# Finishing the last sample unit's pending results in turns

## The chip, the cores and the metric

The kernel runs on one core of one Trainium2 chip. The metric is the device time of one execution in microseconds. Five engines run their own queues, each in order: TensorE (PE, with its weight loads PEld), VectorE (DVE), ScalarE (ACT), GpSimd (POOL) and SyncE (SP). ACT, SP and POOL also issue DMA transfers from their queues.

## The reference

One encoder layer is applied to two sequences with the same weights: a sample of 1024 tokens and a prompt of 512. All is float32.

```python
h = rms_norm(x, norm_g)                 # width 2048
z = h @ w_in                            # 2048 -> 5632: c_val, c_glu, c_gate, q, k, v, a_gate
conv = conformer_conv(c_val, c_glu, ...) * silu(c_gate)   # 31 taps, layer norm, 1024x1024 product
attn = banded_sink_attention(rope(q), rope(k), v, sink) * silu(a_gate)  # 8 heads, window 128
y = rms_norm(x + concat[conv, attn] @ w_out, final_norm_g)
```

A gate's path, which matters here, is short: a product with `w_in`, a scaling by the token's RMS factor, a SiLU, and a store to device memory.

## The kernel before, in words

**Products.** Every float32 product is made of three matmuls on halves: an operand is split into a high part (`hi`, an ACT copy or scaling) and a low part (`lo`, a DVE subtraction), and hi x hi, hi x lo and lo x hi are accumulated. `parts` (L506 to L515) writes such a split. Weights are loaded as `raw` tiles (3 buffers) and split into `hl` tiles (3 buffers); tokens live split in `t` tiles (28 buffers).

**Units, for the sample.** `Unit` (L94) makes two blocks of 128 columns of `w_in` times 1024 tokens over half of the 16 blocks of inputs, in Strassen's way: seven products (steps 0 to 6, order P1, P2, P6, P5, P7, P3, P4) of 4 blocks x 3 matmuls of 128x512 each, so 12 matmuls a step (`product`, L193, matmuls at L207). After a step its sum is taken off PSUM by `tap` (L230); that work is late, that is, it is traced in the next step behind its first three matmuls. Four results come out of a unit, named by token half and column block: (0,0) after P2, (1,1) after P7, (0,1) after P3 and (1,0) after P4.

**Pending results.** A unit over the second half of the inputs must add the partial result of the first half, which waits in device memory. `finish` (L260) issues an accumulating DMA from the POOL queue (`add_into`, L501: tile `g` or `u` <- `part_...`, 256 KB) and appends an entry to the list `later`: a counter, `landing` (4 for most units), and a generator with the rest of the work. For a gate the generator is `silu_of` (L976): first the scaling on DVE (`scaled`, L975), and at the next call the SiLU on ACT (L983) and the store to `gate_d` (L984); for the last gates the store is issued on ACT's own queue. The tiles `g` and `u` have four buffers each and are also used by the rotation of queries and keys, by the attention's query loads (L1150) and others.

**Turns.** `turn_over` (L542) counts down every entry of `later`, and calls the generator of each whose counter has come to zero; one call a turn. In a unit there is a turn in each step, behind the first three matmuls and the late work. `turn_over(True)` calls all of them, whatever their counter. What a turn traces has priority (`high_priority(URGENT)`), so the planner that orders each engine's instructions may put it ahead of up to some 400 instructions traced before it.

**Marks.** `turn_over` also calls `mark` (L523), which remembers the last DVE and the last ACT instruction traced so far. What is traced within `behind` (L534) is queued on those engines behind the marks. All steps of the three background lanes (`conv`, `attn`, `prep`; class `Lane`, L64) run within `behind`: the convolution's taps, the attention, and preparations. Lanes are advanced by `tick`, as time is counted while the matmuls are traced. The order on an engine comes from the planner, by priority and by what it takes to be ready, within these bounds.

**Jobs, for the prompt.** `Job` (L386) makes one block of 128 columns times 512 tokens over 16 blocks of inputs (`k`), 3 matmuls each, so 48 (L670); the jobs with `w_pw` have 8 blocks. `run` (L641) goes through all items: the sample's units, the prompt's 44 jobs (keys and values first, then queries, then convolution and gates), 16 jobs with `w_pw` for the sample, the units with `w_out`, and 8 jobs with `w_pw` for the prompt; a last stage follows. At each half of a job, behind its first three matmuls, the next weights are prepared (`w_prep`) and there is one turn. The late work of the job before comes behind the first three matmuls of a job. Before each job, `later` is emptied by forced turns (L657, L658).

**Around the boundary.** `end` is the sample's last unit with `w_in`, two gate blocks. During its steps 0 to 3 it also splits the prompt's 16 token blocks (`follow`, L2018: an ACT scaling at L514 and a DVE operation at L515 for each, four blocks a step), into the `t` tiles that its own tokens leave. Its `landing` is 8. The prompt's first two jobs make the keys and values of head group 0 (weights split at L510 and L511, or, where the low part was kept in device memory, at L418 and L420), and the sample's attention starts beside them (L1131, L1161, L1169 on).

Of the kernel before, what the change touches and what calls it, by code (L numbers as in the profile page):

```python
# [45 lines left out]
NT, NRAW, NHL = 28, 3, 3  # L46
OWN = 12
FILLS = {(0, 1, 2): 2, (1, 0, 0): 3}
HALF = 4
# [381 lines left out]
class Encoder:  # L431
# [209 lines left out]
    def run(self, items):  # L641

        nc = self.nc
        late = []
        for n, item in enumerate(items):
            for x in item:
                for fn in x.before:
                    fn()
            if isinstance(item[0], Unit):
                for u in item:  # L650
                    u.alone = len(item) == 1
                    u.open()
                for step in range(len(item[0].STEPS)):
                    for u in item:
                        late = u.product(step, late)
                continue
            while self.later:  # L657
                self.turn_over(True)  # L658
            job = item[0]
            job.acc = [self.acc()]  # L660
            nk = len(job.ks)
            for q in range(0, nk, 2 * HALF):
                at = job.at + q // (2 * HALF)
                self.w_prep(at + 1)
                hl = self.hl.pop(at)
                for kk in range(2 * HALF):
                    i = q + kk
                    hi, lo = job.rhs(job.ks[i])
                    for p, (l, r) in enumerate(((0, hi), (0, lo), (1, hi))):
                        nc.tensor.matmul(  # L670
                            job.acc[0],
                            hl[:, l, kk // HALF, kk % HALF, :],
                            r,
                            start=i == 0 and p == 0,
                            stop=i == nk - 1 and p == 2,
                        )
                    if kk == 0:
                        self.w_prep(at + NHL - 1)
                        self.turn_over()
                    if i in job.ticks:  # L680
                        job.ticks[i]()
                    self.tick(3 * MM)
                    if i == 0:
                        for fn in late:
                            fn()
                        late = []
            late = [lambda job=job: self.urgently(job.evac, job.acc)]
        for fn in late:
            fn()
# [1185 lines left out]
def encoder(ctx, tc, a):  # L1875
# [152 lines left out]
            load_two(j)  # L2028

    end = stages[3][-1]  # L2030
    end.look, end.landing = NHL - 1, 8
    end.before.append(last_before)
    for step in range(4):
        end.after[step] = [lambda step=step: follow(step)]
# [143 lines left out]
```

## Time and profile before

| | us |
|---|---|
| runs, median (lowest to highest) | 2078.87 (2078.43 to 2080.28) |
| the profiled execution | 2079.13 |
| its span | 2077.4 |
| PE busy | 2060.1 |
| DVE busy | 1728.4 |
| ACT busy | 1081.8 |
| POOL busy | 157.9 |

The span is the part of the execution that the trace covers; the rest of its time lies around it. A row of a timeline gives the start, the time from the first instruction's start to the last one's end, the engine, the line, the operation, the tiles written and read, their count, and in brackets how long the engine was idle before it and what ended that. SPq, ACTq and POOLq are DMA issues on those queues. Matmuls are pipelined, so that a row of several is longer than their number times the distance between two by the length of one's tail. A row of waits gives engine, line and tile that waited, what it waited for, and the total, the count and the longest, in us.

### The profile page before, as it was taken

What the parts mean: (1) busy time and instruction counts of PE and PEld (TensorE: products, weight loads), DVE (VectorE), ACT (ScalarE), POOL (GpSimd) and SP (SyncE); (2) the same over time, 40 slices, a digit from 0 to 9 for tenths busy, and PEclk for the clock granted to TensorE, in tenths of its full rate; (3) what the DMA queues carried; (4) which work ended last, traced back from release to release, by engine and by line L of the source; (5) the groups of instructions that cost most, each with busy time, mean ns of one, the idle gap of its engine ahead of it and who ended that gap; (6) DMA issues with size and microseconds to landing.
All of it is one profiled execution on the core that took longest, in us unless ns stands there. A gap on an engine that the chain in (4) does not pass through costs nothing.

```text
span 2077.4 us, 27223 instructions
## 1 busy us (share of the span) xinstructions
PE 2060.1 (99%) x9256; PEld 1697.9 (82%) x9256; DVE 1728.4 (83%) x2843; ACT 1081.8 (52%) x1771; POOL 157.9 (8%) x240
## 2 busy tenths in 40 slices
PE   9999999999999999999999999999999999999998
PEld 8888888888888888788888888888888887888886
DVE  8768899998899899889766777776799978998877
ACT  7486445333465555655555777336553343454454
POOL 0111111111112111100000000000000111100000
PEclk9999999999999999999999999999999999999999
DMA  8888886864577777954555555997789898778897
GB/s 285 309 300 256 200 215 226 286 218 158 190 243 197 181 167 179 279 167 158 164 183 185 178 172 188 316 329 233 239 295 295 279 324 283 213 259 277 293 324 279
DMA packets 242300, 494.56 MB, mean 238 GB/s; under 512 B 23664, under 2 KB 84464, under 8 KB 242160
## 3 DMA queue, kind: packets, MB, share of 16 engines
q1 hardware_dynamic: 216352, 428.83, 62.1%
q0 software_dynamic: 24512, 61.88, 12.5%
q10 hardware_dynamic: 1296, 2.11, 0.3%
q8 instruction: 72, 1.18, 0.2%
q14 instruction: 68, 0.56, 0.1%
HBM read 331.77 MB, written 160.96 MB: 237 GB/s over the span
## 4 chain that ended last, share of the span: by engine, by line
PE 73%; issue 8%; DMA 8%; DVE 7%; ACT 2%; POOL 1%; SPq 0%; ACTq 0%; POOLq 0%; DVEq 0%
PE a L207 21%; PE a L670 13%; PE c L207 10%; PE b L670 6%; PE c L670 6%; PE b L207 5%; PE s L1169 2%; PE pv L1198 2%; PE a L1852 2%; PE s L207 2%; DVE hl L511 2%; PE pt L1203 1%; PE s L1852 1%; DVE t L511 1%; DMA p<-y_d 1%
## 5 line engine op out<-in xcount | busy, mean ns | idle before, releaser
L207 PE MATMUL a<-t,hl 128*128 128x512 f32 x2640 | 632.5, 390 | 1.8 <-ACT u L236 1.3
L207 PEld LDWEIGHTS a<-t,hl 128*128 128x128 f32 x2640 | 493.5, 188 | 108.4 <-ACT u L236 2.4
L511 DVE TENSOR_TENSOR hl<-raw,hl 128x1024 fp32r<-128x1024 f32 (+3 forms) x334 | 337.8, 1012 | 151.5 <-ACT hl L510 147.3
L510 ACT ACTIVATE hl<-raw 128x1024 fp32r<-128x1024 f32 (+3 forms) x334 | 296.8, 889 | 314.4 <-PE c L207 88.1
L670 PE MATMUL a<-t,hl 128*128 128x512 f32 x1344 | 326.3, 393 | 0.0
L207 PE MATMUL c<-t,hl 128*128 128x512 f32 x1320 | 319.1, 389 | 0.0
L670 PEld LDWEIGHTS a<-t,hl 128*128 128x128 f32 x1344 | 248.8, 188 | 50.4
L207 PEld LDWEIGHTS c<-t,hl 128*128 128x128 f32 x1320 | 247.4, 188 | 51.5 <-DVE u L304 0.2
L1041 DVE SCALAR_TENSOR_TENSOR f<-f,c_w_dw,f 128x512 f32<-128x512 f32 x248 | 172.9, 744 | 0.2
L670 PE MATMUL b<-t,hl 128*128 128x512 f32 x672 | 162.9, 392 | 1.5 <-DVE t L515 0.8
L670 PE MATMUL c<-t,hl 128*128 128x512 f32 x672 | 163.9, 393 | 0.0
L1004 DVE SCALAR_TENSOR_TENSOR f<-f,c_w_dw,f 128x512 f32<-128x512 f32 x232 | 163.4, 742 | 0.2
L207 PE MATMUL b<-t,hl 128*128 128x512 f32 x660 | 159.8, 389 | 0.0
L670 PEld LDWEIGHTS b<-t,hl 128*128 128x128 f32 x672 | 124.8, 188 | 27.5 <-DVE t L515 1.1
L670 PEld LDWEIGHTS c<-t,hl 128*128 128x128 f32 x672 | 124.6, 188 | 24.8
L207 PEld LDWEIGHTS b<-t,hl 128*128 128x128 f32 x660 | 123.7, 188 | 25.6
L1033 DVE SCALAR_TENSOR_TENSOR f<-f,w_both,f 128x512 f32<-128x512 f32 x120 | 89.8, 748 | 2.0
L236 ACT ACTIVATE u<-a 128x512 f32<-128x512 f32 x82 | 48.8, 595 | 77.3 <-PE a L207 70.6
L236 ACT ACTIVATE g<-a 128x512 f32<-128x512 f32 x78 | 46.5, 596 | 78.5 <-PE a L207 68.5
L1183 ACT ACTIVATE p<-p,tiny 128x384 f32<-128x384 f32 (+1 forms) x96 | 54.6, 570 | 45.9 <-DVE tiny L1180 36.2
L510 ACT ACTIVATE a<-pt 128x512 fp32r<-128x512 f32 x64 | 38.0, 593 | 64.6 <-PE pt L1203 64.4
L285 POOL DMA_DIRECT2D g<-xT_s x16 | 8.8, 551 | 743.1 <-DMA att_d<-u 669.0
(356 smaller groups left out, 2765.2 us busy)
## 6 DMA issues: line engine op xcount, KB each, us to landing
raw<-w_in SPq DMA_DIRECT2D x170, 512.0 KB, 5.2
raw<-w_out SPq DMA_DIRECT2D x31, 512.0 KB, 5.1
raw<-w_pw SPq DMA_DIRECT2D x24, 512.0 KB, 4.2
wsum_P<-raw SPq DMA_DIRECT2D x47, 256.0 KB, 3.6
raw<-wsum_P SPq DMA_DIRECT2D x18, 512.0 KB, 5.1
f<-x_s SPq DMA_DIRECT2D x16, 512.0 KB, 8.5
g<-wsum_P SPq DMA_DIRECT2D x28, 256.0 KB, 4.6
a<-sum_S SPq DMA_DIRECT2D x24, 256.0 KB, 6.1
```

The costliest lines, as they stand in the source:

```text
L207: nc.tensor.matmul(acc, hl[:, l, o, j, :], toks[j][:, r], start=name in FRESH and j == 0 and q == 0, stop=name in LAST and j == HALF - 1 a ...
L236: nc.scalar.activation(t, bank, AF.Copy)
L510: nc.scalar.activation(hi, x, AF.Copy)
L511: nc.vector.tensor_tensor(lo, x, hi.bitcast(F32), ALU.subtract)
L670: nc.tensor.matmul(job.acc[0], hl[:, l, kk // HALF, kk % HALF, :], r, start=i == 0 and p == 0, stop=i == nk - 1 and p == 2,)
L1004: nc.vector.scalar_tensor_tensor(t, h[:, j : j + T], w(j), t, ALU.mult, ALU.add)
L1033: nc.vector.scalar_tensor_tensor(m0, odd[:, j : j + H], both(j), m0, ALU.mult, ALU.add)
L1041: nc.vector.scalar_tensor_tensor(out, d[:, j : j + H], w(2 * j + k), out if j else m0, ALU.mult, ALU.add)
L1169: nc.tensor.matmul(ps[:, 0:n], qs[:, x, h], k[y][:, keys], start=p == 0, stop=p == 2)
L1183: nc.scalar.activation(p[:, 0:n], p[:, 0:n], AF.Exp, bias=nm[:, h : h + 1], accum_out=l[:, h : h + 1])
L1198: nc.tensor.matmul(pv, v[x][:, vs], pt[:, y], start=i == 0 and p == 0, stop=i == last and p == 2)
L1852: nc.tensor.matmul(acc[t], self.toks[name, m][:, x, i, t * P : (t + 1) * P], parts[i][l].rearrange("p a b -> p (a b)"), start=fresh and fi ...
```

## The change

Three lines change. The forced turns before each job go. In a job there is a turn at every fourth block of inputs, where before there was one at every eighth. And the `landing` of the sample's last unit becomes 5 in place of 8. What is pending when a job begins stays in `later` and is finished in that job's or the next one's turns.

```diff
@@ def run
                         late = u.product(step, late)
                 continue
-            while self.later:
-                self.turn_over(True)
             job = item[0]
             job.acc = [self.acc()]
...
                     if kk == 0:
                         self.w_prep(at + NHL - 1)
+                    if kk % HALF == 0:
                         self.turn_over()
                     if i in job.ticks:
                         job.ticks[i]()
@@ def encoder
     end = stages[3][-1]
-    end.look, end.landing = NHL - 1, 8
+    end.look, end.landing = NHL - 1, 5
     end.before.append(last_before)
```

`HALF` is 4. The loop `for kk in range(2 * HALF)` runs over the eight blocks of a half of a job.

## The prediction

> **What bounds the kernel now.** I read the page's busy shares first, then the busy time by stretches, because the change touches one place in the middle.
>
> ```profile
> span 2077.4 us, 27223 instructions
> PE 2060.1 (99%) x9256; PEld 1697.9 (82%) x9256; DVE 1728.4 (83%) x2843; ACT 1081.8 (52%) x1771; POOL 157.9 (8%) x240
> ```
> ```profile
> 856.00:870.00 14.00, 12.55 (x53) 9.52 (x52) 8.34 (x11) 8.61 (x12) 0.88 (x1) 1.00 1.05 318
> 870.00:900.00 30.00, 30.00 (x146) 24.92 (x145) 22.08 (x45) 16.82 (x30) 0.00 (x0) 1.00 0.60 196
> 900.00:1000.00 100.00, 100.00 (x472) 82.92 (x471) 90.38 (x164) 53.35 (x101) 0.00 (x0) 1.00 0.50 164
> 1200.00:1400.00 200.00, 198.66 (x912) 162.99 (x911) 145.13 (x247) 104.60 (x163) 0.00 (x0) 1.00 0.74 250
> 1800.00:1910.00 110.00, 110.00 (x490) 90.61 (x489) 99.51 (x154) 56.51 (x86) 5.50 (x10) 1.00 0.77 254
> ```
>
> The columns are the stretch, its length, then PE, PEld, DVE, ACT, POOL busy, the granted clock and the DMA's share and rate. TensorE is the bound nearly everywhere. Its one marked hole in the middle is 856 to 870 us, where the prompt's first job runs: 14.00 - 12.55 = 1.45 us. The timeline of PE shows it in steps.
>
> ```profile
> 833.63 5.60 PE L207 MATMUL a<-t,hl 128*128 128x512 f32 x24
> 839.07 2.88 PE L207 MATMUL b<-t,hl 128*128 128x512 f32 x12
> ...
> 856.03 0.61 PE L670 MATMUL b<-t,hl 128*128 128x512 f32 x2
> 857.14 10.67 PE L670 MATMUL b<-t,hl 128*128 128x512 f32 x44 [0.49 <-DVE hl L511]
> 868.63 0.73 PE L670 MATMUL b<-t,hl 128*128 128x512 f32 x2 [0.82 <-DVE t L515]
> 869.20 6.30 PE L670 MATMUL a<-t,hl 128*128 128x512 f32 x27
> ```
>
> Undisturbed, 24 matmuls take 839.07 - 833.63 = 5.44 us, 0.2267 us each. The first job's 48 should take 10.88 us and take 869.20 - 856.03 = 13.17: 2.29 us lost. Of that, 1.11 - 0.45 = 0.66 us goes at the start, for the first weight's low part (L511), and the other 1.63 us later, mostly for the last token split (L515). The chain of waits tells why that split is late.
>
> ```profile
> 855.03 6.64 DMA u<-part_gate
> 861.68 0.03 issue
> 861.70 0.70 DVE u L975
> 862.40 0.02 issue
> 862.43 0.64 ACT u L983
> ...
> 864.12 0.90 ACT hl L418
> ...
> 865.71 0.96 ACT hl L510
> ...
> 867.83 0.76 DVE t L515
> ```
>
> So the 256 KB accumulating load of a pending result, issued at 855.03, lands at 861.67. The scaling on DVE (L975) and the Silu on ACT (L983) stand in the queues in front of the splits. DVE and ACT show the rest.
>
> ```profile
> 857.00 0.68 DVE L975 TENSOR_TENSOR g<-g,f 128x512 f32<-128x512 f32 x1
> 860.18 0.69 DVE L975 TENSOR_TENSOR u<-u,f 128x512 f32<-128x512 f32 x1 [2.50 <-DMA u<-part_gate]
> 861.70 0.69 DVE L975 TENSOR_TENSOR u<-u,f 128x512 f32<-128x512 f32 x1 [0.83 <-DMA u<-part_gate]
> 862.31 0.75 DVE L515 SCALAR_TENSOR_TENSOR t<-a,c_norm_g,t 128x512 fp32r<-128x512 f32 x1
> ...
> 869.63 0.68 DVE L975 TENSOR_TENSOR g<-g,f 128x512 f32<-128x512 f32 x1
> ```
> ```profile
> 860.91 0.63 ACT L983 ACTIVATE u<-u 128x512 f32<-128x512 f32 x1 [2.56 <-DVE u L975]
> 862.43 0.63 ACT L983 ACTIVATE u<-u 128x512 f32<-128x512 f32 x1 [0.89 <-DVE u L975]
> 863.19 0.89 ACTq L984 DMA_DIRECT2D gate_d<-u  x2
> 865.61 1.04 ACT L510 ACTIVATE hl<-raw 128x1024 fp32r<-128x1024 f32 x1
> 866.56 0.71 ACT L514 ACTIVATE t<-a,c_norm_g 128x512 fp32r<-128x512 f32 x1
> ```
>
> DVE idles 2.50 + 0.83 = 3.33 us on the two landings, ACT 3.45 us behind it, and ACT then issues two stores (0.89 us). The last split's ACT half starts only at 866.56.
>
> **The change part by part.** *The forced finish goes.* In place of two rounds at the job's start, the results come in turns, one every 12 matmuls, and the first, (0,0), reaches its fifth turn in the unit's last step. Its scaling stands behind the first weight's low part, where it is at 857.00 already: cost 0, and the 0.66 us at the start stay. (1,1) is scaled at the ninth k of job 0, 22 matmuls behind 857.14, 862.1 us; its load had landed by 860.18. (0,1) comes 12 matmuls on, at 864.8, landed by 861.67. (1,0), with a load issued a little later, comes in the second job, after 870, where 869.63 showed no wait. Three scalings (0.69 us), three Silus (0.63) and their stores on ACT's own queue move behind the splits; none is added. What was queued behind them, the last splits, needs 0.75 us of DVE each and can be done before 861, while PE wants the last at matmul 46, near 866.9. Gain: the 1.63 us.
>
> *What is late next.* The second job starts at 857.14 + 46 x 0.2267 = 867.57 instead of 869.20, so its weights (L510 at 865.61, then 1.23 us of L511) must keep up. If L418 still starts at 864.12, L511 ends near 867.9, and the third matmul wants it at 868.02. That weight goes into the buffer that job 0's first half frees at 862.1, so no earlier. I take off 0.2 us for this, bounds 0 (L418 earlier) and 1.63 (job 2 not ready before 869.20): net gain 1.4, between 0 and 1.6. I stay near the upper end because the Silu and store issue, 0.63 + 0.89 us, no longer stand before L418.
>
> *Buffers.* The waiting results hold their u and g tiles some 5 to 7 us longer. Of four u tiles two are held, one is the query's and one the rotation's; the next query load (SP) wants one when the first query has been read. If it had to wait, the weight loads behind it on SP would slip by up to 3 us, but the third job's weight has more margin than that.
>
> ```profile
> 865.83 0.69 DVE L511 TENSOR_TENSOR a<-u,a 128x512 fp32r<-128x512 f32 x1
> 875.95 1.23 DVE L511 TENSOR_TENSOR hl<-raw,hl 128x1024 fp32r<-128x1024 f32 x1 [2.31 <-ACT hl L510]
> 881.70 5.61 PE L670 MATMUL c<-t,hl 128*128 128x512 f32 x24
> ```
>
> The low part ends at 877.18 and PE wants it at 881.70 or, with the gain, 880.3: 3 us of cover. Cost 0; without the cover the whole slip, up to 3 us.
>
> *The marks.* Every turn also renews the point behind which the background lanes (convolution, attention, preparation) are ordered. The 44 prompt jobs have two halves, the 24 later ones one: 112 turns become 224. No instruction is added; the order on DVE and ACT tightens in all jobs. No trace shows its price. From below: nothing, or a gain up to the idle PE has left between 900 and 1910 us, of which the row 1200 to 1400 has the most, 1.34 us. From above, see the slower rival. I take 0, since 1800 to 1910 has DVE 90% busy and no idle PE.
>
> *Other pending results.* The second sample stage's last output squares also lose their forced finish; they need one turn only, and PE is full there (1800 to 1910): 0.
>
> *The sum.* The profiled execution took 2079.13 us, 1.73 around its span. 2079.13 - 1.4 = 2077.7; the runs' median, 2078.87, is 0.26 lower: **2077.5 us**.
>
> **A rule against the trace.** The loads above took 6.6 to 7 us from issue to landing. The Trainium skill, DMA: Bandwidth & Descriptors, Anatomy of one DMA, fits 2.0 us plus bytes over 436e3 per us for this path; an estimate from that page for 262,144 bytes is 2.6 us. By that rule both loads would have landed by 857.7, the forced finish would wait for nothing, and the change would bring nothing, 2078.9. The DVE rows disagree: 860.18 and 861.70.
>
> **The rivals.** *The wait stays (2078.9).* Turns are urgent: the planner may put a scaling ahead of its turn, if it thinks the load has landed, and a split behind it again. For: the mark alone fixes how early, and (1,1) has only 862.1 - 860.18 = 1.9 us in hand. Against: it now stands behind the second job's weight, which is late itself. Gain 0 to 0.4.
>
> *The lanes are pinned (slower).* Attention's parts between transposes and products have no margin:
>
> ```profile
> 1017.89 0.60 PE L1203 MATMUL pt<-c_ident,p 128*128 128x128 f32 x4
> 1019.71 0.93 PE L1198 MATMUL pv<-a,t 128*128 128x512 f32 x3
> ```
> ```profile
> 1018.52 0.60 ACT L510 ACTIVATE a<-pt 128x512 fp32r<-128x512 f32 x1 [2.85 <-PE pt L1203]
> ```
> ```profile
> 1019.16 0.69 DVE L511 TENSOR_TENSOR a<-pt,a 128x512 fp32r<-128x512 f32 x1 [0.78 <-ACT a L510]
> ```
> ```profile
> L1041 DVE SCALAR_TENSOR_TENSOR f<-f,c_w_dw,f 128x512 f32<-128x512 f32 x248 | 172.9, 744 | 0.2
> ```
> ```profile
> L1203 PE MATMUL pt<-c_ident,p 128*128 128x128 f32 x256 | 42.8, 274 | 0.2
> ```
>
> DVE ends the low part at 1019.85, and the products begin at 1019.71. If the new mark forces one convolution tap (0.744 us) in front, PE waits that long. There are 256 / 4 = 64 such groups, half of them behind the new marks: 32 x 0.744 = 23.8 us if none is covered; with half covered 11.9, hence 2077.5 + 11.9 = 2089. It passes 0.2% from eight uncovered groups on: 8 x 0.744 - 1.4 = 4.6 us. Against: DVE idles 0.78 us before this very part, so taps are done by then, and the planner can put job matmuls ahead.
>
> *The last Silu falls behind the first Exp.* ACT holds one table until attention's first Exp, and (1,0)'s Silu moves from 870.34 towards it:
>
> ```profile
> 870.34 0.63 ACT L983 ACTIVATE g<-g 128x512 f32<-128x512 f32 x1 [0.35 <-DVE g L975]
> 875.94 1.28 ACT L1183 ACT_TABLE_LOAD   x1
> 879.43 0.51 ACT L1183 ACTIVATE p<-p,tiny 128x256 f32<-128x256 f32 x1 [2.21 <-DVE tiny L1180]
> ```
>
> Its turn is the second job's ninth k, 867.57 + 24 x 0.2267 = 873: before the Exp. From 879.4 on, it costs two table loads, 2 x 1.28 = 2.57 us of ACT. With ACT 53% busy between 900 and 1000 they are hidden: 2077.5; bare, 2080.1. The Trainium skill, ScalarE: Activation LUTs, What ACT_TABLE_LOAD costs, counts 2.66 us a switch with its drain; by an estimate from that page ACT loses 5.3 us. The trace agrees on the load itself, 1.28 us.
>
> *The order shifts well elsewhere:* PE's small idles shrink, 2075 to 2077.
>
> **How the numbers follow.** A measurement of this kernel tells about 0.2%, 4.2 us, from no change. Chances: forecast 0.54 (2076.8 to 2078.2); the wait stays 0.16 (2078.5 to 2079.5); lanes pinned 0.15, of which 0.11 over 4.2 us slower; Exp 0.05; order elsewhere 0.10, of which 0.07 over 4.2 us faster, if it reaches the tail too. So faster 0.07, within 0.82, slower 0.11. The range reaches from 2075.2, a full gain and an idle of some 2 us more, to 2081.3, past the bare table loads and into the pinned lanes.
>
> **What would show it.** Right: L975 without a wait for part_gate; the last L514 and L515 before 862; job 1 starting 11.5 us behind job 0; DVE and ACT counts unchanged. Wrong: L975 waiting 1 us or more; a second Silu table load near 880; waits of PE or PEld at L1198 summing to several us between 900 and 1700. A time under 2074.7 or over 2083 would mean that the renewed marks, not the finish, decide.

## The result, and the profile after

The changed kernel takes **2086.80 us** (median of 6 runs, 2084.43 to 2092.08), the kernel before beside it 2080.05 (6 runs, 2078.43 to 2081.45): a ratio of **1.0040, 95% interval 1.0029 to 1.0051** (the quotient of the medians, 1.0032, lies inside it). The forecast was 2077.5 us and a range to 2081.3, so the prediction is wrong, in sign too. The profiled execution after took 2086.7 us, with a span of 2084.9, 7.5 us above the span before. Behind L657 the changed kernel's lines are two lower, behind L676 one lower: L670 is now L668, L975 is L974, L983 is L982, L1169 is L1168, L1198 is L1197.

The first two lines of the page after show the same work as before: equal counts on PE, DVE and ACT, and their busy times within 2 us.

```profile
span 2084.9 us, 27230 instructions
PE 2061.8 (99%) x9256; PEld 1695.4 (81%) x9256; DVE 1728.7 (83%) x2843; ACT 1083.2 (52%) x1771; POOL 158.0 (8%) x240
```

So no work was added. Of the 7.5 us PE is busy for 1.7 and idle for 5.8. The busy time by stretches says where; the columns are those of the prediction's table.

```profile
856.00:870.00 14.00, 13.50 (x60) 10.86 (x59) 9.04 (x12) 8.26 (x12) 0.88 (x1) 1.00 1.01 309
1200.00:1400.00 200.00, 197.95 (x904) 161.88 (x903) 144.44 (x240) 105.22 (x160) 0.00 (x0) 1.00 0.73 249
1400.00:1600.00 200.00, 194.25 (x888) 158.75 (x887) 160.04 (x288) 103.01 (x189) 7.75 (x14) 1.00 0.77 250
1600.00:1800.00 200.00, 197.41 (x883) 161.51 (x882) 175.23 (x279) 82.46 (x138) 21.41 (x39) 1.00 0.89 291
1800.00:1910.00 110.00, 110.00 (x489) 90.60 (x489) 101.60 (x157) 56.15 (x84) 6.05 (x11) 1.00 0.76 250
```

Two of these stretches in the kernel before:

```profile
1400.00:1600.00 200.00, 199.59 (x917) 164.45 (x915) 165.95 (x290) 105.95 (x190) 7.75 (x14) 1.00 0.80 264
1600.00:1800.00 200.00, 199.05 (x891) 163.76 (x892) 176.56 (x280) 82.49 (x139) 21.95 (x40) 1.00 0.88 283
```

At the boundary PE idles less, 14.00 - 13.50 = 0.50 us in place of 1.45. Far behind it, where no pending result is touched, it idles more: 5.75 in place of 0.41 us between 1400 and 1600, 2.59 in place of 0.95 between 1600 and 1800. The granted clock is 1.00 in all these rows.

**The boundary.** The timelines of PE, DVE and ACT of the changed kernel:

```profile
856.00 0.61 PE L668 MATMUL b<-t,hl 128*128 128x512 f32 x2
857.11 10.73 PE L668 MATMUL b<-t,hl 128*128 128x512 f32 x46 [0.50 <-DVE hl L511]
867.68 6.29 PE L668 MATMUL a<-t,hl 128*128 128x512 f32 x27
```
```profile
856.97 0.69 DVE L974 TENSOR_TENSOR g<-g,f 128x512 f32<-128x512 f32 x1
...
864.67 0.69 DVE L974 TENSOR_TENSOR g<-g,f 128x512 f32<-128x512 f32 x1 [0.96 <-DMA g<-part_gate]
865.28 0.74 DVE L515 SCALAR_TENSOR_TENSOR t<-a,c_norm_g,t 128x512 fp32r<-128x512 f32 x1
865.95 1.22 DVE L511 TENSOR_TENSOR hl<-raw,hl 128x1024 fp32r<-128x1024 f32 x1
867.08 1.29 DVE L974 TENSOR_TENSOR u<-u,f 128x512 f32<-128x512 f32 x2
```
```profile
863.10 0.72 ACT L514 ACTIVATE t<-a,c_norm_g 128x512 fp32r<-128x512 f32 x1
...
874.29 0.62 ACT L982 ACTIVATE g<-g 128x512 f32<-128x512 f32 x1
...
875.29 1.28 ACT L1182 ACT_TABLE_LOAD   x1 [0.39 <-ACT g L982]
```

Job 0 takes 867.68 - 856.00 = 11.68 us where it took 13.17: 1.49 us gained. The wait for `hl` at its start is still there, and the second wait, for the last split, is gone. The scalings have moved behind the splits (two of `u` at 867.08), with one exception: the planner put (1,0)'s scaling of `g` ahead of them, where it waits 0.96 us for its own load with the last split behind it. That split ends at 866.02, soon enough.

**Where it went.** For a table by stage I took the start of the same product matmul (before's lines L207, L349, L670, L1806 and L1852, counted from the first; 8412 of them in each trace) in two traces and subtracted. Plus is lost, minus is gained, us, one profiled execution each.

| stretch, in the time of before | after |
|---|---|
| 5 to 860, sample units | 0.0 |
| 860 to 912, jobs 0 to 3 | -2.0 |
| 912 to 1439, the other prompt jobs | +4.8 |
| 1439 to 1539, 16 `w_pw` jobs | +0.1 |
| 1539 to 1563, first `w_out` unit | +4.7 |
| 1563 to 1609 | -0.8 |
| 1609 to 1694 | +0.9 |
| 1694 to 1734 | +2.1 |
| 1734 to 1870 | 0.0 |
| 1870 to 2067 | -2.0 |

Two rows need care. Four of attention's transposes (0.56 us) run before 912 in the kernel before and behind it in the changed one, so job 0 alone makes 1.4 of the 2.0 us gained, and 4.2 of the 4.8 us lost are left. The last row is no gain of the change: -1.6 to -2.2 us stand there in every variant below but e5 (+5.2). Between 1911 and 1930 the profiled execution of before had a granted clock of 0.91, where the others have 1.00 in that stage but for e5, and the same 45 matmuls took it 1.92 us longer (stretch and matmuls before, then the matmuls after):

```profile
1911.00:1930.00 19.00, 18.94 (x85) 15.53 (x84) 15.80 (x32) 10.72 (x17) 0.00 (x0) 0.91 0.77 248
```
```profile
1912.55 12.41 PE L1852 MATMUL a<-hl,t 128*128 128x512 f32 x45
```
```profile
1922.23 10.49 PE L1851 MATMUL a<-hl,t 128*128 128x512 f32 x45
```

Without that, these two traces differ by 7.5 + 1.9 = 9.4 us.

The most concentrated loss is 4.7 us in one unit, behind 1539. These are the rows of PE that idle there, and PE's waits between 1538 and 1575 (total, count, longest); the kernel before shows none in that window.

```profile
1545.47 0.75 PE L1168 MATMUL s<-f,a 128*128 128x256 f32 x4 [1.44 <-DVE a L511]
...
1558.80 0.96 PE L207 MATMUL c<-t,hl 128*128 128x512 f32 x3 [0.87 <-DVE t L511]
1560.40 1.42 PE L207 MATMUL a<-t,hl 128*128 128x512 f32 x5 [0.64 <-ACT t L510]
...
1563.49 0.60 PE L1202 MATMUL pt<-c_ident,p 128*128 128x128 f32 x4
...
1568.60 0.51 PE L1197 MATMUL pv<-a,f 128*128 128x512 f32 x1 [1.31 <-ACT a L510]
```
```profile
PE s L1168 <- DVE a L511: 1.4, 1, 1.4
PE pv L1197 <- ACT a L510: 1.3, 1, 1.3
PE c L207 <- DVE t L511: 0.9, 1, 0.9
PE a L207 <- ACT t L510: 0.6, 1, 0.6
PE a L207 <- DVE u L304: 0.4, 1, 0.4
```

Together these are 4.6 us, the loss of the unit, and the granted clock is 1.00. PE waits for everything by turns: attention's splits, token splits, an operand sum. What they share is the head of the queue of ACT and of DVE. First ACT after, then DVE after, then the same subtraction on DVE before:

```profile
1544.60 0.63 ACT L510 ACTIVATE t<-f 128x512 fp32r<-128x512 f32 x1 [3.46 <-DMA f<-msum_S]
...
1566.39 0.63 ACT L510 ACTIVATE t<-f 128x512 fp32r<-128x512 f32 x1 [3.27 <-DMA f<-mix_d]
1566.93 0.61 ACT L510 ACTIVATE hl<-raw 128x512 fp32r<-128x512 f32 x1
1567.45 0.61 ACT L510 ACTIVATE hl<-g 128x512 fp32r<-128x512 f32 x1
1567.97 0.58 ACT L510 ACTIVATE a<-pt 128x512 fp32r<-128x512 f32 x1
```
```profile
1537.38 0.69 DVE L143 TENSOR_TENSOR g<-raw,raw 128x512 f32<-128x512 f32 x1 [4.35 <-DMA mix_d<-g]
```
```profile
1531.90 0.69 DVE L143 TENSOR_TENSOR g<-raw,raw 128x512 f32<-128x512 f32 x1 [1.43 <-DMA mix_d<-g]
```

At 1566.39 ACT has stood 3.27 us with a token split whose tokens had not landed, and two weight splits and attention's `a<-pt`, which PE wants, stand behind it. The Trainium skill, TensorE: Matmul & The Clock Gate, Architectural detail, calls the queues of ACT and DVE strictly first in, first out; the trace agrees: the transposes that `a<-pt` reads ended at 1564.09, it starts at 1567.97, and PE's `pv` (L1197) starts 1.31 us late, at 1568.60.

### The profile page after: what moved, and what is told of

It is laid out like the page before. It is cut to its first block, busy times and chain, and to the rows that moved or that the text cites. A ratio compares the mean times of both kernels' runs of the same rounds, so it can differ in the third digit from the quotient of the medians.

```text
span 2084.9 us, 27230 instructions
## 1 busy us (share of the span) xinstructions
PE 2061.8 (99%) x9256; PEld 1695.4 (81%) x9256; DVE 1728.7 (83%) x2843; ACT 1083.2 (52%) x1771; POOL 158.0 (8%) x240
## 5 line engine op out<-in xcount | busy, mean ns | idle before, releaser
L207 PE MATMUL a<-t,hl 128*128 128x512 f32 x2640 | 632.8, 390 | 3.7 <-DVE u L304 1.5
L207 PEld LDWEIGHTS a<-t,hl 128*128 128x128 f32 x2640 | 493.5, 188 | 110.9 <-ACT t L510 2.6
L510 ACT ACTIVATE hl<-raw 128x1024 fp32r<-128x1024 f32 (+3 forms) x334 | 297.0, 890 | 329.9 <-PE c L207 79.4
L511 DVE TENSOR_TENSOR hl<-raw,hl 128x1024 fp32r<-128x1024 f32 (+3 forms) x334 | 338.3, 1013 | 138.2 <-ACT hl L510 136.5
L668 PE MATMUL a<-t,hl 128*128 128x512 f32 x1344 | 326.7, 393 | 1.2 <-DVE hl L511 1.2
L207 PE MATMUL c<-t,hl 128*128 128x512 f32 x1320 | 320.4, 390 | 0.9 <-DVE t L511 0.9
L668 PEld LDWEIGHTS a<-t,hl 128*128 128x128 f32 x1344 | 248.7, 188 | 51.6 <-DVE hl L511 2.0
L207 PEld LDWEIGHTS c<-t,hl 128*128 128x128 f32 x1320 | 247.1, 188 | 53.3 <-DVE t L511 1.7
L668 PE MATMUL c<-t,hl 128*128 128x512 f32 x672 | 165.4, 394 | 0.9 <-ACT hl L510 0.6
L668 PE MATMUL b<-t,hl 128*128 128x512 f32 x672 | 162.9, 392 | 0.5 <-DVE hl L511 0.5
L207 PE MATMUL b<-t,hl 128*128 128x512 f32 x660 | 160.0, 390 | 0.0
L668 PEld LDWEIGHTS b<-t,hl 128*128 128x128 f32 x672 | 125.0, 188 | 25.6 <-DVE hl L511 0.9
L668 PEld LDWEIGHTS c<-t,hl 128*128 128x128 f32 x672 | 124.4, 188 | 25.6 <-ACT hl L510 0.8
L207 PEld LDWEIGHTS b<-t,hl 128*128 128x128 f32 x660 | 123.7, 188 | 25.5
L511 DVE TENSOR_TENSOR a<-pt,a 128x512 fp32r<-128x512 f32 x64 | 44.1, 689 | 37.6 <-ACT a L510 37.2
L510 ACT ACTIVATE a<-pt 128x512 fp32r<-128x512 f32 x64 | 38.0, 594 | 67.7 <-PE pt L1202 67.3
```

What stands on the lines that cost most here:

```text
L207: nc.tensor.matmul(acc, hl[:, l, o, j, :], toks[j][:, r], start=name in FRESH and j == 0 and q == 0, stop=name in LAST and j == HALF - 1 a ...
L510: nc.scalar.activation(hi, x, AF.Copy)
L511: nc.vector.tensor_tensor(lo, x, hi.bitcast(F32), ALU.subtract)
L668: nc.tensor.matmul(job.acc[0], hl[:, l, kk // HALF, kk % HALF, :], r, start=i == 0 and p == 0, stop=i == nk - 1 and p == 2,)
```

## The experiments

Every ratio is against runs of the kernel before on the same chip, with a 95% interval. Medians of before in these sets were 2076.45 to 2077.74 us. Costs in us are worked out from the ratios. The expectations stand as they were recorded; lines in the experiments' kernels are up to four higher than before's. A name such as e1 is a run's: e1 to e8 are experiments 1 to 8, e9 and e10 the two engines of 9 and 10, f2 is 11, f1 12, f3 13 and g1 14.

**1. The marks alone.** The kernel before with the added marks and nothing else: forced finish, turns and `landing` as they were.

```diff
                         self.w_prep(at + NHL - 1)
                         self.turn_over()
+                    if kk == HALF:
+                        self.mark()
```

> The kernel before, with one thing of the change added: the marks are renewed at every fourth block of a job too. The forced finish and the landing of 8 stay. Theory A (the renewed marks cost the time): the loss is here without the gain at the boundary, about 6.75 + 1.5 = 8 us slower than before, ratio 1.003 to 1.005, with PE falling behind between 1340 and 1420, 1540 and 1580 and 1710 and 1745 us as in the changed kernel, and job 0 still taking 13.2 us. Theory B (the finish in turns reorders what follows and that costs the time): no change, ratio 0.999 to 1.001. Theory C (any reordering of the lanes costs some us): slower, but at other places than in the changed kernel.

Measured: 2087.80 us, ratio 1.0058 (1.0044 to 1.0071). The marks alone cost 0.0058 x 2077.33 = 12 us (10.5 by the medians). By the stage table e1 loses 4.3 us at 912 to 1439, 3.8 at 1539 to 1563 and 2.6 at 1694 to 1734: the places of the changed kernel.

**2. The turns alone.** The changed kernel, whose added turns count and finish but don't renew the marks.

```diff
-    def turn_over(self, all=False):
+    def turn_over(self, all=False, fresh=True):
 
-        self.mark()
+        if fresh:
+            self.mark()
...
                     if kk % HALF == 0:
-                        self.turn_over()
+                        self.turn_over(fresh=kk == 0)
```

> The changed kernel, but the added turn at the fourth block of a half counts and finishes pending results without renewing the marks. Theory A: the gain alone, 1 to 2 us faster than before, ratio 0.9990 to 0.9996, job 0 in 11.5 us. Theory B: as slow as the changed kernel, ratio 1.003 to 1.005. Theory C: slower by some us at other places.

Measured: 2075.22 us, 0.9993 (0.9985 to 1.0002). That is 0.0007 x 2077.33 = 1.5 us under before, the gain that was forecast (1.4), though the interval also holds no change. The two runs make the result within the intervals: 1.0058 x 0.9993 = 1.0051, beside 1.0040 (1.0029 to 1.0051).

**3. An added turn only where something is pending.**

```diff
-                    if kk % HALF == 0:
+                    if kk == 0 or kk == HALF and self.later:
                         self.turn_over()
```

> The changed kernel, but the added turn is made, with its marks, only while something is pending, so in the prompt's first two jobs and at the start of the last eight. Theory A: the 42 other prompt jobs have their old marks, so the gain alone, 1 to 2 us faster than before, ratio 0.9990 to 0.9996. Theory B: as slow as the changed kernel, ratio 1.003 to 1.005. Theory C: slower by some us, at other places.

Measured: 2074.47 us, 0.9987 (0.9979 to 0.9996): faster than both kernels. So marks in the few jobs that have a result to finish are harmless, and what costs is renewing them in jobs that have nothing pending.

**4. The marks moved, not added.** Before's one turn of each half goes from the first to the fifth block.

```diff
                     if kk == 0:
                         self.w_prep(at + NHL - 1)
+                    if kk == HALF:
                         self.turn_over()
```

> The kernel before, with its one turn and mark in each half of a job moved from the first block to the fifth: as many marks as before, elsewhere. The forced finish and the landing of 8 stay. Theory A in its tight form (more marks leave the lanes less room): no change, ratio 0.999 to 1.001. Theory A in its loose form (a mark that falls on a lane's own instruction, not on the weights', does the harm): slower by 4 us or more, ratio 1.002 or above. Theory B: no change. Theory C: slower, at other places than the changed kernel.

Measured: 2082.10 us, 1.0023 (1.0013 to 1.0032). The same 112 marks at another place cost 4.8 us, so it isn't their number alone. The place of the loss is the changed kernel's: e4 loses 3.6 us in the first `w_out` unit and 1.3 at 1694 to 1734.

**5. Four marks a half.**

```diff
                         self.turn_over()
+                    elif kk % 2 == 0:
+                        self.mark()
```

> The kernel before with the marks renewed at every second block of a job, four times a half; the forced finish stays. If the loss grows with the number of marks (theory A, tight), it is larger than with two marks a half (ratio 1.0058): 1.008 to 1.015. If what matters is that a mark falls on a lane's own instruction at all (theory A, loose), about the same: 1.003 to 1.007. If any reordering costs by chance (theory C), anything from 0.999 to 1.008, with the losses at other places than with two.

Measured: 2104.35 us, 1.0125 (1.0111 to 1.0138), 26 us. By the stage table 14.0 of its 27.6 us go at 912 to 1439, and the largest single wait of PE between 1340 and 1400 is for a job's weight:

```profile
PE b L670 <- DVE hl L511: 5.8, 1, 5.8
```

**6 and 7. Which jobs.** The added marks in the 24 `w_pw` jobs alone (first line), or in the 44 prompt jobs alone (second).

```diff
+                    if kk == HALF and nk == NC:
+                        self.mark()
```
```diff
+                    if kk == HALF and nk == ND:
+                        self.mark()
```

> The kernel before with the added marks in the 24 jobs with w_pw alone, which run from about 1440 to 1540 us and from 1870 us on. If the 4.7 us that PE loses right behind 1540 come from the marks just before them, the ratio is 1.0015 to 1.0030. If they come from what the lanes fell behind in the prompt's 44 jobs, no change: 0.999 to 1.001.

> The kernel before with the added marks in the prompt's 44 jobs alone, 856 to 1440 us. The other half of the run before: 1.002 to 1.0035 if the places are independent (the losses of 3.5 us up to 1440 alone), 1.004 to 1.006 if the loss behind 1540 and the one near 1720 are carried over from here.

Measured: 2084.76 us, 1.0031 (1.0019 to 1.0042), for the `w_pw` jobs; 2082.23 us, 1.0020 (1.0011 to 1.0029), for the prompt jobs. 24 marks cost 6.4 us, 88 cost 4.2, and together they make e1's 12 within the intervals. The stage table sets them apart: the prompt's marks lose 4.6 us at 912 to 1439 and none (-0.2) in the first `w_out` unit, the others lose 5.2 us in that unit and nothing (-1.0) at 912 to 1439. So a mark can be paid for where it isn't set: the `w_pw` jobs themselves lose nothing (1439 to 1539: 0).

**8. A mark on another instruction.** The added mark stands behind a job's late work, on its evacuation, where the fifth block's stands on whatever was traced last.

```diff
                         for fn in late:
                             fn()
+                        if late:
+                            self.mark()
                         late = []
```

> The kernel before with one more mark in each job, taken right behind the late work of the job before, so that it falls on that job's own last instruction (the evacuation) and not on a lane's. If a mark harms only where it falls on a lane's own instruction, no change: 0.999 to 1.001. If any added mark harms because lanes have less room to run ahead, slower: 1.002 to 1.006, and then PE falls behind between 1340 and 1440 and behind 1540 again.

Measured: 2086.31 us, 1.0042 (1.0029 to 1.0054). So a mark behind the evacuation costs as well. It doesn't show that what a mark stands on is indifferent: the evacuation of a `w_pw` job uses DVE alone (L1533), so ACT's mark still stood on whatever was traced last. The losses lie elsewhere: 2.1 us at 912 to 1439, 0.9 in the first `w_out` unit, 4.1 at 1563 to 1609.

**9 and 10. Which engine.** The added marks renew one engine's point only (for ACT, `Activation` in place of `DVE`).

```diff
-    def mark(self):
+    def mark(self, only=None):
...
+        if only:
+            found = {**{i.engine: i for i in self.marks}, only: found[only]}
         self.marks = list(found.values())
...
+                    if kk == HALF:
+                        self.mark(mybir.EngineType.DVE)
```

> The kernel before with the added marks in all jobs, as in the run with 1.0058, but for DVE alone: ACT's mark stays the one of the half's first block. If the order on DVE is what costs (DVE is 79 to 88% busy where PE falls behind, ACT 41 to 53%), nearly the whole loss: 1.004 to 1.006. If it is ACT's order, 0.999 to 1.001. If either will do, 1.002 to 1.004.

> The kernel before with the added marks in all jobs for ACT alone; DVE's mark stays the one of the half's first block. Marks for both gave 1.0058 and for DVE alone 1.0032. If the two engines' orders cost independently, the rest: 1.0015 to 1.0035. If DVE's order alone decides and the difference was scatter, 0.999 to 1.001. If either order alone is enough, 1.003 to 1.006.

Measured: DVE alone 2084.10 us, 1.0032 (1.0020 to 1.0045); ACT alone 2085.41 us, 1.0041 (1.0027 to 1.0055). Each alone costs over half of e1's 0.0058, and neither is free. Whether the two add isn't decided: 0.0032 + 0.0041 = 0.0073 is not clear of e1's interval (0.0044 to 0.0071) with the scatter of its own. That the lanes pass each item through both engines, so that holding one holds the other, would fit and is argued.

**11. Fewer marks, same turns.** Experiment 2 with a mark only at a job's first block, 44 fewer than before.

```diff
-                        self.turn_over()
+                        self.turn_over(fresh=i == 0)
```

> The changed kernel's turns without added marks (that gave 0.9993), and in the prompt's 44 jobs the mark only at the first half, so 44 marks fewer than before. If the lanes gain from room to run ahead, faster still: 0.997 to 0.999. If the marks of before already leave enough, the same as without: 0.9985 to 1.0000. If lanes that run too far ahead take DVE from the weights, slower: over 1.001.

Measured: 2075.27 us, 0.9997 (0.9988 to 1.0006). So not every other order is dearer: taking marks away costs nothing and gains nothing.

**12. One tile's wait.** In 6, DVE waits for the store `mix_d <- g` at L143, because a `g` tile is still being stored. Here the first `w_out` unit writes that difference to a `u` tile.

```diff
-            t2 = self.e.G([HALF, P]) if self.side or not self.total else self.e.A([HALF, P], F32)
+            room = self.e.U if self.spare else self.e.G
+            t2 = room([HALF, P]) if self.side or not self.total else self.e.A([HALF, P], F32)
...
+    over[0][0].spare = True
```

> The kernel before with the added marks in the 24 w_pw jobs, as in the run with a ratio of 1.0031, and one more edit: the first w_out unit's difference (line 143) goes to a u tile instead of a g tile. Theory D: the marks keep the lanes from running ahead, and the lost lead (in that run 3 taps and 2 token splits fewer done when the w_out units begin) costs PE time only because DVE is then held 4 us by this instruction, which waits for a g tile that a store of a gate result still reads. Then the 5.2 us that PE lost between 1540 and 1565 go, and the ratio falls to 1.0000 to 1.0015. If the lost lead alone costs it, the loss stays: 1.0025 to 1.004.

Measured: 2082.80 us, 1.0029 (1.0020 to 1.0039), as without it. The wait for the store went, and DVE idled as long for ACT, which idled for a load of token sums (ACT, then DVE; L511 and L512 here are before's L510 and L511):

```profile
1531.85 1.94 ACT L511 ACTIVATE t<-f 128x512 fp32r<-128x512 f32 x3 [6.16 <-DMA f<-msum_S]
```
```profile
1536.14 0.69 DVE L512 TENSOR_TENSOR hl<-raw,hl 128x512 fp32r<-128x512 f32 x1 [4.53 <-ACT hl L511]
```

The tile was not the cause; this theory falls.

**13. The same tile in the best version.** Experiment 3 with the edit of 12.

> The added turn and mark only while something is pending (0.9987), and the u tile for the first w_out unit's difference. The kernel before waited 1.43 us on DVE at that place and PE lost nothing marked there, so theory D expects no more than 1 us of further gain: 0.998 to 0.999. If the u tile is itself late (the lanes' attention uses u tiles), slower than 0.9995.

Measured: 2078.12 us, 1.0003 (0.9994 to 1.0012). No gain, if anything a loss beside experiment 3 (0.9979 to 0.9996), which stays the best.

**14. The lead given back.** The wait for token sums suggested that the lanes come late to the `w_out` units. I counted, at the last matmul before the first `w_out` unit (number 6218), how many convolution taps (`f<-f,c_w_dw,f` and `f<-f,w_both,f`) and token splits (`t<-f,t`) DVE had begun:

| kernel | taps | splits | lost at 1539 to 1563, us |
|---|---|---|---|
| before | 562 | 37 | |
| e2 | 562 | 37 | +1.4 |
| f2 | 562 | 37 | -0.1 |
| e7 | 562 | 37 | -0.2 |
| e3 | 562 | 37 | +0.7 |
| f3 | 562 | 39 | +1.5 |
| after | 559 | 34 | +4.7 |
| e4 | 559 | 34 | +3.6 |
| e5 | 559 | 34 | +4.0 |
| e1 | 559 | 35 | +3.8 |
| e6 | 559 | 35 | +5.2 |
| e10 | 559 | 35 | +3.9 |
| e8 | 559 | 35 | +0.9 |
| e9 | 561 | 35 | +2.1 |
| f1 | 560 | 35 | +6.3 |

All with the lead of before lose at most 1.5 us there, and nearly all without it lose 2 to 6 us; e8 loses its 4.1 just behind. The two groups are told apart by the code too: all in the lower one, and none in the upper one, have a mark later in a `w_pw` job of the sample than before's. That covers e4, whose marks only move. Experiment 14 is experiment 6 with the preparation lane at 1.5 times its rate from the filling of the mix until the `w_out` units.

```diff
                 e.prep.add(mix.fill())
+                e.prep.rate = 1.5
...
         e.prep.drain()
+        e.prep.rate = 1.0
```

> The kernel before with the added marks in the 24 w_pw jobs (1.0031), and the preparation lane at a rate of 1.5 instead of 1.0 from the second eight w_pw jobs until the w_out units begin, so that the w_out units' token splits are traced earlier. Theory D, second form: the marks cost the w_out token splits their lead over PE, and late splits, waiting for their own loads on ACT (12.2 us on the loads of token sums between 1520 and 1575, against 7.0 before), hold up attention and weights behind them. Then the lead given back takes most of the 5.2 us between 1540 and 1565 away: ratio 1.000 to 1.0015, and the wait on those loads falls to 9 us or less. If the marks harm through the order itself, whatever the lead, the loss stays: 1.0025 to 1.004.

Measured: 2085.99 us, 1.0042 (1.0029 to 1.0054). The lead came back (562 taps, 39 splits), and the loss at 1539 to 1563 went (-0.4 us beside 5.2). ACT's waits between 1520 and 1575 for the token sums, in the order before, e7, e6, after (e2 has 7.6 us, e1 15.0; g1 has no such row):

```profile
ACT t L510 <- DMA f<-msum_S: 7.0, 5, 3.0
```
```profile
ACT t L510 <- DMA f<-msum_S: 7.3, 5, 3.7
```
```profile
ACT t L510 <- DMA f<-msum_S: 12.2, 7, 4.1
```
```profile
ACT t L510 <- DMA f<-msum_S: 13.1, 7, 4.3
```

But the time did not fall: 5.3 us are lost in the next stretch, 1563 to 1609, nearly all at one place. DVE and PE of g1:

```profile
1593.65 0.69 DVE L304 TENSOR_TENSOR u<-a,u 128x512 f32<-128x512 f32 x1 [3.24 <-DMA u<-xT_s]
```
```profile
1594.49 4.29 PE L207 MATMUL a<-t,hl 128*128 128x512 f32 x12 [3.33 <-DVE u L304]
```

Another urgent operation now stands at the head of DVE's queue with a load that hasn't landed, and PE waits 3.33 us for it. Most of the rest of the 5.3 us is the clock's: the 12 matmuls behind the wait take 4.29 us where 12 take 2.88 elsewhere, and the granted clock, 1.00 before and after, falls to 0.70 here:

```profile
1594.40:1600.00 5.60, 5.51 (x19) 4.43 (x20) 4.25 (x7) 0.00 (x0) 0.00 (x0) 0.70 1.01 392
```

The lead cured a second place too: at 1694 to 1734 g1 loses nothing (-0.2), where after, e1, e6, e8, e9, e10 and f1 lose 2.0 to 3.6 us. So the late lanes go with the loss in the first `w_out` unit, and curing them doesn't cure the time. Whether the marks or the higher rate made the new wait isn't shown, since no run has the rate without the marks.

## Why the prediction was wrong

- **"The forced finish goes"**, gain 1.63, net 1.4: right. Job 0 gained 1.49 us, the 0.66 us at its start stayed (857.11 - 856.00 - 0.45 = 0.66), and the runs without the added marks gained 1.5 (e2) and 2.7 us (e3).
- **The times of the three scalings**: half right. I had (1,1) at 862.1 and (0,1) at 864.8 without a wait, and the last splits done by 861. Instead (1,0)'s came first, at 864.67, and waited 0.96 us, and those two came together at 867.08; the last split was half done at 863.10 and done at 866.02. This is the step that the rival "the wait stays" doubted, and as it said, the planner moved a scaling ahead of its turn. It cost nothing, since PE wanted the split near 867.
- **"What is late next"**, 0.2 us: nothing was. The second job's weight ended at 865.95 + 1.22 = 867.17, and the job started at 867.68 without a wait.
- **Buffers**, 0: right as far as the time shows; jobs 0 to 3 gained 2.0 us together, 0.56 of it by the moved transposes, and lost nothing behind job 0.
- **"The marks … I take 0"**: this is the step that failed. It measured +12 us alone (e1), and 0.0040 + 0.0007 = 0.0047 of 2080 us, near 10, inside the change. My reason, that 1800 to 1910 has DVE 90% busy and no idle PE, was read from the wrong stretch: of 1800 to 1910 only the part from 1870 on, the prompt's `w_pw` jobs, has added marks, and PE is 110.00 busy of 110.00 there after the change too. The other added marks stand between 856 and 1539, with the losses among them and right behind. My bound from below, a gain of the idle that PE had left, says nothing on what new idle may come.
- **Other pending results**, 0: right; 1734 to 1870 gained and lost nothing, and from 1870 on the changed kernel stands like e1 and e7, which keep the forced finish (-2.0, -2.1 and -1.9, the clock of before's execution).
- **The slower rival** named the cause, renewed marks holding the lanes, at 0.15, with 2089 us. It had the wrong place. It expected a convolution tap in front of each of 32 groups of attention between transposes and products. The weight load's waits at those products (between 900 and 1700 us, before and then after) grew by 5.7 + 3.4 - 4.1 - 1.8 = 3.2 us, from 22 waits to 34 with the same mean of 0.27 us; the rival had priced 32 of 0.744 us each. Matmuls waited there once, 1.3 us, behind the late load of 1566.39, and once in before, 0.6 us:

```profile
PEld pv L1198 <- DVE a L511: 4.1, 14, 1.0
PEld pv L1198 <- ACT a L510: 1.8, 8, 0.3
```
```profile
PEld pv L1197 <- ACT a L510: 5.7, 20, 1.7
PEld pv L1197 <- DVE a L511: 3.4, 14, 0.4
```

  So its cause was right, and that its 2089 came near the time is luck: it priced that place at 11.9 us, and the matmuls there idled 0.7 us more. Its sign, waits at L1198 summing to several us, could not tell either, as they sum to 5.9 us in the kernel before.
- **The Silu behind the first Exp**: did not happen. The Silu of `g` started at 874.29, the table load for Exp at 875.29, 1.28 us as before and no second one.
- **What would show it wrong**: "over 2083 would mean that the renewed marks, not the finish, decide". That was the right test, and experiments 1 to 3 bear it out.

**What stays open.** Shown are: that renewed marks in jobs with nothing pending make the whole loss; that marks in the `w_pw` jobs take some three taps and two or three splits of lead from the lanes; and that with the lead given back the waits in the first `w_out` unit go, and those near 1716. That the late lanes issue their loads later, so that these stand unlanded at the head of ACT's queue, fits the rows (7.0 to 13.1 us of waits) and is argued, not tried by itself. Not tied to one cause are the 2 to 5 us between 912 and 1439 (after, e1, e7, e8, e10; e9 loses 0.4): in the changed kernel only 1.6 us of them are idle times of PE over 0.15 us (2.9 in place of 1.3), the others shorter gaps. Open too are the 4 to 5 us at 1563 to 1609 of e8 and g1. Traces of single executions also differ by -1 to +3 us over the first 860 us, where all kernels run the same work, so terms of 1 us in the stage tables carry no weight.

## What to carry to other kernels

A bookkeeping call that renews an ordering point has a price of its own in every round in which there is nothing to do: call it only when something is pending (0.9987 in place of 1.0040 here). When a change multiplies such a point, don't price it by how full the bound engine is; count at the same matmul how far the background work has come, and ask which load its next instruction will wait for at the head of the queue.

## What was not expected of the hardware

- An instruction that waits for a load at the head of ACT's or DVE's queue holds unrelated, urgent work for as long as 6.16 us (`f<-msum_S`, f1), with ACT 52% busy over the span. I had read a half-idle engine as cover.
- When one such wait went, another came 50 us later (5.2 us at 1539 to 1563 in e6, 5.3 at 1563 to 1609 in g1), and the total did not fall.
- A wait of PE can cost more than its own length. In the sixteen traces PE idles for over 2.2 us nine times between 50 and 1950 us, and behind seven of these the granted clock fell to 0.50 for 2 us or more (e5 after 5.85 us of idle, g1 after 3.33, e1 after 2.45); behind two it did not (3.23 in e9, 2.57 in e10). Of sixteen idles of 1.3 to 2.2 us two were followed by it. The changed kernel's trace has no such fall, so its loss is waiting alone.
- The same instructions in the same order between 0 and 860 us took from 1 us less to 2.9 us more in one profiled execution than in another, more than the 1.5 us which the change's own step brings.
